# Three tiles begun at two changes of phase, norms' small products at fixed places, and the SSD's first group with its gates ahead of B and C

## The chip, the cores and the metric

The kernel runs on one core of a Trainium2 chip. The metric is the device time of one execution in microseconds (us); lower is better. A core has TensorE (PE, matrix products into PSUM), VectorE (DVE), ScalarE (ACT), GpSimd (POOL) and SyncE (SP), which issues the DMAs here. Each engine has a queue of its own and runs it in order; semaphores hold an instruction until what it reads is there.

## The reference

A backbone of two layers on 512 latent tokens and 256 context tokens, 1024 channels. Layer 0 mixes with attention, layer 1 with a bidirectional Mamba-2 state-space mixer (SSD); behind each comes a gated ConvFFN. Cut to what matters:

```python
for i in range(2):
    h_l = modulate(rms_norm(x, norm_mix_w[i]), mod_l[0], mod_l[1])      # the same for ctx
    o_l, o_c = attention_mixer(h_l, h_c, ...) if i == 0 else mamba2_mixer(h_l, h_c, ...)
    x = x + mod_l[2] * o_l                                              # ctx too in layer 0
    h_l = modulate(rms_norm(x, norm_ffn_w[i]), mod_l[3], mod_l[4])
    x = x + mod_l[5] * conv_ffn(h_l, ...)                               # ctx too in layer 0

def conv_ffn(h, w_up, conv_w, conv_b, w_down):
    g, u = jnp.split(h @ w_up, 2, axis=-1)
    g = dwconv_centred(g, conv_w, conv_b)
    return (jax.nn.silu(g) * u) @ w_down

# in mamba2_mixer
z, xbc, dt = jnp.split(h @ w_in, [D_INNER, D_INNER + CONV_DIM], axis=-1)
xbc = jax.nn.silu(dwconv_centred(xbc, conv_w, conv_b))                  # x, B and C
dt_f = jax.nn.softplus(dt_f + dt_bias_f)                                # dt_b likewise
# in ssd_scan, per chunk of 128 tokens
acs = jnp.cumsum(dtc * a, axis=2)
decay_end = jnp.exp(acs[:, :, -1:] - acs)
xw = xc * (decay_end * dtc)[..., None]
states = jnp.einsum('bcsgn,bcsgrp->bcgrpn', bc, xw)
```

## The kernel before, in words

Activations lie with channels on the partitions: a tile is 128 channels by tokens, and 1024 channels make 8 k-tiles. Tokens come in three segments: the context (256 columns), and the first and the second half of the latents (256 each). All products are float32 in three terms: activations and weights are split into a high half (`hh`, `wh`) and a low half (`hl`, `wl`), and `mm3` (L100) issues wh x hh (L105), wh x hl (L106) and wl x hh (L108) into one PSUM tile. A weight of 128 x 1024 is loaded by `load_w`: a DMA of 512 KB on SP's queue into `wst`, a cast on ScalarE that makes `wh` (L85), a subtraction on VectorE that makes `wl` (L87). `wst`, `wh` and `wl` share ten buffers, so a weight can be asked for only when an older one has been used up.

PSUM is cut into two tiles of 1024 columns (`S`) and four banks of 512 columns (`Bank`). GEMMs use `S`; down projections, the norms' small products and the first group's small steps use banks in turn.

A framework orders the instructions of each engine by its own estimate of when each is ready, program order deciding between equals; the queues then run in that order.

At a **change of phase** the last down projection of one phase (`down`, L952), the norm behind it (`Norm`, L345 on), and the first GEMMs of the next phase meet. For each segment and each of 8 output tiles m, `down` issues the products `ps_d` and a VectorE step X (L970) that adds gate times product to the residual; `Norm.sq` squares the new X on ScalarE and adds the squares. When a segment's eight are done, `Norm.gen` (L383) runs beside the next segment: the product with ones `ss` (L267), `rsa` on VectorE (L270), Ln and Exp on ScalarE (L272), two small steps `rsu` (L274, L275) and the row `rb` on VectorE (L278), then its transpose on TensorE (`rsT`, L284) and a copy `rs` on ScalarE (L394). Then `modulated` makes for each k-tile `ht` on VectorE (L312), the high half on ScalarE and the low half `hl` on VectorE (even k-tiles, L322) or, with two ScalarE steps, on GpSimd (odd ones, L317 to L319). `first_tiles` (L438) begins the two first GEMM tiles of the next phase in the two `S` tiles (`ps_first`): context and first latent half together, k by k for one tile and then the other, then the second half. Two such changes use it: from attention to layer 0's ConvFFN, whose first tiles are gate tile 0 and the up tile that goes with it (names ending in f), and from that ConvFFN to the SSD, whose first are the time steps dt and x tile 0 (names ending in s).

In the ConvFFN (`ffn`, L982) gate tile 1 is a GEMM of its own, 512 and 256 columns, in two banks (`ps_up1`).

The **SSD** (`ssd`, L1068) makes acs and dt from the first tile: Abs and Relu on ScalarE (L1106, L1107), then a chain on VectorE of exponentials' sums, a reciprocal, products and four scans (L1110 to L1128). It works in eight groups of six GEMMs (`inproj`): x, x, B, C, z, z. x, B and C are copied by ScalarE into a buffer `raw`, and go through a five-tap conv, four taps on VectorE (`xf`, `Bf`, `Cf`, L1152), and a Silu. Each group's state and outputs (`core`) are cut into steps that are taken while the next GEMMs run. Behind group 0's C come the transposes of acs and dt (`ps_dtT`, copied by VectorE into `acsT`, `dtT`, L1328), the product `ps_end` (L1333) that spreads each chunk's last value, and what hangs on them (`dec`, `dw`, `nacs`).

At the SSD's end `late_first` (L449) begins ConvFFN 1's first tiles behind the output projection with `Norm.chain`, which has one lag for both of its waits.

## Time and profile before

| what | us |
|---|---|
| median of 3 runs | 1902.2 (1901.54 to 1905.32) |
| the profiled execution | 1906.4 |
| its span | 1904.2 |
| TensorE busy in the span | 1864.1 |
| VectorE busy | 1331.0 |
| ScalarE busy | 845.4 |
| GpSimd busy | 256.9 |

The span runs from the first to the last instruction of the profiled execution. A row of the timeline gives start, duration, engine, line, operation, output and inputs; in square brackets stands the idle time of the engine ahead of it and what ended it. A row of a group ends with the same idle time summed. Products are pipelined: one of 256 columns is shown as 0.28 us, and the next starts before it ends. The mean granted clock of TensorE was 0.994 of full speed.

### The profile page before, as it was taken

The numbers are of one execution on the slowest core, as the hardware profiler recorded it, in microseconds if no ns is written. First come the engines' busy times: TensorE is split into PE (matmuls) and PEld (weight loads), VectorE is DVE, ScalarE is ACT, GpSimd is POOL, SyncE is SP. The second block draws the span as 40 slices with busy tenths as digits, with TensorE's granted clock in tenths as the row PEclk, the third lists the DMA queues.
The fourth block names the chain that finished last, engine by engine and source line by source line (L and its number), as shares of the span: only waits on it lengthen the run. The fifth ranks groups of instructions, "written<-read, shape, count | busy, mean of one in ns | idle before, by whom it ended". The sixth has DMA issues, their size and how long they took to land.

```text
span 1904.2 us, 27262 instructions
## 1 busy us (share of the span) xinstructions
PE 1864.1 (98%) x10696; PEld 1528.8 (80%) x10696; DVE 1331.0 (70%) x1983; ACT 845.4 (44%) x1454; POOL 256.9 (13%) x238
## 2 busy tenths in 40 slices
PE   8899999989999999999999999999999999999999
PEld 6774545578888888888888888888888888888887
DVE  4478889678877777544478777777878576565555
ACT  3645544355122222222256767766677352323331
POOL 2300000031000000000040334443334200000000
PEclk8999999999999999999999999999999999999999
DMA  9123341014334556221222344344343323323332
GB/s 339 56 67 97 118 157 40 23 56 166 122 122 133 163 189 186 72 67 56 67 89 80 116 122 122 114 131 123 116 130 119 100 78 101 101 86 111 89 99 89
DMA packets 73424, 210.00 MB, mean 110 GB/s; under 512 B 8912, under 2 KB 14416, under 8 KB 73168
## 3 DMA queue, kind: packets, MB, share of 16 engines
q1 hardware_dynamic: 73296, 208.26, 35.1%
q8 instruction: 84, 1.38, 0.3%
q14 instruction: 44, 0.36, 0.1%
HBM read 198.79 MB, written 6.82 MB: 108 GB/s over the span
## 4 chain that ended last, share of the span: by engine, by line
PE 79%; DVE 9%; issue 3%; ACT 3%; DMA 1%; POOL 1%; SPq 0%; DVEq 0%; POOLq 0%; ACTq 0%
PE ps_up L105 10%; PE ps_up L106 10%; PE ps_up L108 10%; PE ps_d L105 6%; PE ps_d L108 6%; PE ps_d L106 6%; PE ps_in L108 4%; PE ps_in L106 4%; PE ps_in L105 4%; PE ps_o L760 2%; PE ps_s L796 2%; PE ps_st L1222 2%; DVE ht L312 1%; PE ps_wo L108 1%; PE ps_wo L105 1%
## 5 line engine op out<-in xcount | busy, mean ns | idle before, releaser
L87 DVE TENSOR_TENSOR wl<-wst,wh 128x1024 fp32r<-128x1024 f32 x209 | 260.3, 1245 | 227.7 <-PE ps_up L106 121.6
L85 ACT CAST wh<-wst 128x1024 fp32r<-128x1024 f32 x211 | 221.2, 1049 | 422.0 <-DMA wst<-in_wup 321.6
L106 PE MATMUL ps_up<-hlf,wh 128*128 128x512 f32 x1008 | 357.2, 354 | 0.0
L108 PE MATMUL ps_up<-hhf,wl 128*128 128x512 f32 x1008 | 356.9, 354 | 0.0
L105 PE MATMUL ps_up<-hhf,wh 128*128 128x512 f32 x1008 | 356.7, 354 | 0.0
L105 PEld LDWEIGHTS ps_up<-hhf,wh 128*128 128x128 f32 x1008 | 190.6, 189 | 26.5
L106 PEld LDWEIGHTS ps_up<-hlf,wh 128*128 128x128 f32 x1008 | 190.7, 189 | 26.3
L108 PEld LDWEIGHTS ps_up<-hhf,wl 128*128 128x128 f32 x1008 | 190.6, 189 | 26.4
L105 PE MATMUL ps_in<-hhs,wh 128*128 128x512 f32 (+1 forms) x560 | 204.5, 365 | 0.0
L106 PE MATMUL ps_in<-hls,wh 128*128 128x512 f32 (+1 forms) x560 | 199.5, 356 | 0.0
L108 PE MATMUL ps_in<-hhs,wl 128*128 128x512 f32 (+1 forms) x560 | 198.8, 355 | 0.0
L105 PE MATMUL ps_d<-hdh,wh 128*128 128x512 f32 (+1 forms) x568 | 193.6, 343 | 1.4 <-DVE X L970 1.2
L108 PE MATMUL ps_d<-hdh,wl 128*128 128x512 f32 (+1 forms) x568 | 193.4, 341 | 0.0
L106 PE MATMUL ps_d<-hdl,wh 128*128 128x512 f32 (+1 forms) x568 | 193.0, 340 | 0.3 <-DVE hdl L87 0.3
L970 DVE SCALAR_TENSOR_TENSOR X<-ps_d,mod,X 128x512 f32<-128x512 f32 (+1 forms) x224 | 125.0, 584 | 34.1 <-PE ps_d L108 33.8
L106 PEld LDWEIGHTS ps_d<-hdl,wh 128*128 128x128 f32 x568 | 106.7, 188 | 14.8 <-DVE hdl L87 0.7
L105 PEld LDWEIGHTS ps_d<-hdh,wh 128*128 128x128 f32 x568 | 106.3, 188 | 14.8 <-DVE X L970 1.4
L105 PEld LDWEIGHTS ps_in<-hhs,wh 128*128 128x128 f32 x560 | 106.0, 189 | 15.1 <-issue 0.9
L108 PEld LDWEIGHTS ps_in<-hhs,wl 128*128 128x128 f32 x560 | 105.9, 189 | 14.8
L108 PEld LDWEIGHTS ps_d<-hdh,wl 128*128 128x128 f32 x568 | 106.7, 188 | 13.1
L106 PEld LDWEIGHTS ps_in<-hls,wh 128*128 128x128 f32 x560 | 106.0, 189 | 13.2
L799 ACT ACTIVATE pr<-ps_s 128x1024 f32<-128x1024 f32 x56 | 57.1, 1020 | 94.0 <-PE ps_s L798 86.7
(355 smaller groups left out, 3506.4 us busy)
## 6 DMA issues: line engine op xcount, KB each, us to landing
wst<-in_wup SPq DMA_DIRECT2D x88, 512.0 KB, 3.6
wada<-in_adaT SPq DMA_DIRECT2D x56, 512.0 KB, 3.7
wst<-in_win SPq DMA_DIRECT2D x48, 512.0 KB, 3.7
wst<-in_wdown SPq DMA_DIRECT2D x44, 512.0 KB, 3.7
E<-ad SPq DMA_DIRECT2D x64, 256.0 KB, 6.7
wada<-in_adaB SPq DMA_DIRECT2D x24, 512.0 KB, 5.0
ec<-ead SPq DMA_DIRECT2D x64, 128.0 KB, 5.1
wst<-in_wout SPq DMA_DIRECT2D x16, 512.0 KB, 3.6
```

The lines of the kernel that those rows point to most:

```text
L85: keep(nc.scalar.copy(hi, src))
L87: keep(eng.tensor_tensor(lo, src, _r(hi), ALU.subtract))
L105: mm(out, wh, ah, start=first, stop=False)
L106: mm(out, wh, al, start=False, stop=False)
L108: mm(out, wl, ah, start=False, stop=last)
L312: nc.vector.scalar_tensor_tensor(t[:, c0:c1], ap, g.moda[layer][ca][:, m, v : v + 1], rs[:, c0:c1], ALU.mult, ALU.mult)
L760: nc.tensor.matmul(po[S64[e], :n], v, pr[:, 512 * e + off : 512 * e + off + n], start=first, stop=last)
L796: nc.tensor.matmul(outs[e], a[S64[e], k], b[S64[e], q], start=i == 0, stop=False)
L799: nc.scalar.activation(pr, ps, AF.Exp)
L970: nc.vector.scalar_tensor_tensor(ap, o[:, c0:c1], gate[:, m, v : v + 1], ap, ALU.mult, ALU.add)
L1222: nc.tensor.matmul(ps[:, d * 256 : (d + 1) * 256], Bt[:, t * P : (t + 1) * P], xw[d][t], start=t == ts[0], stop=t == ts[-1])
```

## The change

1. `three_first` takes the place of `first_tiles`. Three tiles are begun: the two of before and gate tile 1 (ConvFFN 0) or x tile 1 (SSD), in two banks (`ps_first1`), whose weight is asked for at its start. It goes segment by segment, context first, and within a segment tile by tile. The last segment's norm runs in it by `Norm.chain`, its `ss` behind six k-steps and its `rsT` behind nine more, held there by `ordered` (an order without a semaphore). The rows of the latent halves are all made with the low half on VectorE.
2. `down` with a norm puts two output tiles into one bank (`ps_dn`), 256 columns each. The context's norm is as before; the first latent half's is a `chain` with a lag of 3 and 3.
3. `ffn` takes gate tile 1 from `first`.
4. `ssd`: dt's relu moves to VectorE (L1144) and Abs goes in three pieces; x tiles 0 and 1 are copied by `taken` at once. Group 0 runs z, z, then the transposes (`turned`), B's GEMM with `ends` behind its fourth k, x's taps, B's conv, C. Its `core` begins with one step and gives the others to group 1.
5. `Norm.chain` gets a second lag `then` (2 where nothing is given).

The core of the diff:

```diff
+def three_first(g, ws, norm, x, third):
+    ctx, la, lb = ending(norm.streams)
+    ws = ws + [load_w(g, third)]
+    tiles = [S(g, "ps_first") for _ in range(2)]
+    tiles = [[t[:, :L], t[:, L:T]] for t in tiles] + [[None, None]]
+    last = [None]
+    chain = norm.chain(LAST, 6, 9, lambda: last[0])
+    todo = {ctx: norm.rows(la, x), la: norm.rows(lb, x), lb: iter(())}
+    for seg in (ctx, la, lb):
+        i, a, b = seg
+        n = 0
+        for ps, w in zip(tiles, ws):
+            if ps[i] is None:
+                ps[i] = Bank(g, "ps_first1")[:, : (L, C)[i]]
+            for k in range(KT):
+                ks = slice(k * P, (k + 1) * P)
+                last[0] = mm3(g, (w[0][:, ks], w[1][:, ks]), [(ps[i][:, a:b], tuple(t[:, a:b] for t in norm.h[i][k]))],
+                              k == 0, k == KT - 1)
+                next(chain, None)
...
@@ down
-            ps = [(i, a, b, Bank(g, f"ps_d{i}")[:, : b - a]) for i, a, b in group]
+            if norm:
+                if m % 2 == 0:
+                    bank = Bank(g, "ps_dn")
+                ps = [(*group[0], bank[:, m % 2 * C : m % 2 * C + C])]
...
-            bg = norm.gen(group[0], x, 2)
-    return bg
+            bg = norm.gen(group[0], x, 2) if group[0][0] else norm.chain(group[0], 3, 3, lambda: last[0]) if group[0] != LAST else iter(())
@@ ssd, inproj
+        if gi == 0:
+            for j in range(2):
+                G.z.append(t2("z"))
+                nc.scalar.copy(G.z[j], gemm(ld(4 + j), (0,))[0])
+            turned()
+            ps = gemm(ld(2), (1, 0), ends)
+            G.x = [taps(*x) for x in x0]
...
+            G.B = conv(ps, 8 * 2, True, t3(g, "Bf"))
+            G.C = conv(gemm(ld(3), (0,)), 8 * 3, False, t2("Cf"))
```

What it moves, in the order of the instructions of an engine (a row: place, line, operation, output and inputs, shape).

TensorE in the second latent half of the down projection at the first change of phase; hhol and hlol are the attention's output, hhf_0 and on the normed k-tiles. Before:

```order
1486 L105 MATMUL ps_d_3961<-hhol_3588,wh 128x256
1487 L106 MATMUL ps_d_3961<-hlol_3589,wh 128x256
1488 L108 MATMUL ps_d_3961<-hhol_3588,wl 128x256
1489 L267 MATMUL ssf_3975<-ones,sqf_3890 128x1 x2
1490 L105 MATMUL ps_first<-hhf_0_3612,wh 128x256
1491 L106 MATMUL ps_first<-hlf_0_3613,wh 128x256
1492 L105 MATMUL ps_first<-hhf_0_3612,wh 128x256
1493 L106 MATMUL ps_first<-hlf_0_3613,wh 128x256
1494 L105 MATMUL ps_d_3988<-hhol_3220,wh 128x256
```

and now:

```order
1473 L108 MATMUL ps_dn<-hhol_3588,wl 128x256
1474 L105 MATMUL ps_first<-hhf_0_3612,wh 128x256
1475 L106 MATMUL ps_first<-hlf_0_3613,wh 128x256
1476 L108 MATMUL ps_first<-hhf_0_3612,wl 128x256
1477 L105 MATMUL ps_first<-hhf_1_3614,wh 128x256
1478 L106 MATMUL ps_first<-hlf_1_3615,wh 128x256
1479 L108 MATMUL ps_first<-hhf_1_3614,wl 128x256
1480 L105 MATMUL ps_first<-hhf_2_3616,wh 128x256
1481 L106 MATMUL ps_first<-hlf_2_3617,wh 128x256
1482 L108 MATMUL ps_first<-hhf_2_3616,wl 128x256
```

Where four products of the first tiles stood between two banks of the down projection, 21 stand now (rows 1474 to 1494), on k-tiles 0 to 6.

VectorE behind that down projection; `wl` is the third weight's low half now, the next GEMM's before, `rbf` the last segment's row. Before:

```order
461 L381 TENSOR_TENSOR sqf_4055<-sqf_4055,sqf_3945 128x256
462 L312 SCALAR_TENSOR_TENSOR ht<-X,moda_99,rsf_4016 128x256 x3
463 L322 SCALAR_TENSOR_TENSOR hlf_4_3605<-ht,mod_89,hhf_4_3604 128x256
464 L270 TENSOR_SCALAR rsa<-ssf_4119 128x2
465 L87 TENSOR_TENSOR wl<-wst,wh 128x1024
466 L322 SCALAR_TENSOR_TENSOR hlf_6_3609<-ht,mod_89,hhf_6_3608 128x256
467 L274 TENSOR_TENSOR rsu<-rsy,rsa 128x2
468 L275 SCALAR_TENSOR_TENSOR rsu<-rsy,rsu 128x2
469 L278 SCALAR_TENSOR_TENSOR rbf_4130<-rsu,rsy 128x256
```

and now:

```order
441 L322 SCALAR_TENSOR_TENSOR ht<-X,moda_99,rsf_4032 128x256
442 L389 TENSOR_TENSOR sqf_4030<-sqf_4030,sqf_4047 128x256
443 L391 TENSOR_TENSOR sqf_4030<-sqf_4030,sqf_3937 128x256
444 L332 SCALAR_TENSOR_TENSOR hlf_0_3597<-ht,mod_89,hhf_0_3596 128x256
445 L279 TENSOR_SCALAR rsa<-ssf_4084 128x2
446 L87 TENSOR_TENSOR wl<-wst,wh 128x1024
447 L283 TENSOR_TENSOR rsu<-rsy,rsa 128x2
448 L284 SCALAR_TENSOR_TENSOR rsu<-rsy,rsu 128x2
449 L287 SCALAR_TENSOR_TENSOR rbf_4095<-rsu,rsy 128x256
```

The norm's steps come behind one k-tile of the first latent half instead of most of them, and a `wl` still stands between `rsa` and `rsu`. On TensorE 14 products now lie between that norm's `ss` and its `rsT`.

VectorE at the SSD's start, from the last scans of acs to the copy of its transpose; `xf` rows are taps of the conv. Before:

```order
979 L1128 SCALAR_TENSOR_TENSOR acs<-dtu,dte 32x384
980 L1152 SCALAR_TENSOR_TENSOR xf<-raw_9259,par,xf 128x770
981 L87 TENSOR_TENSOR wl<-wst,wh 128x1024
982 L1152 SCALAR_TENSOR_TENSOR xf<-raw_9259,par,xf 128x770
983 L1152 SCALAR_TENSOR_TENSOR xf<-raw_9260,par,xf 128x770
984 L1152 SCALAR_TENSOR_TENSOR xf<-raw_9259,par,xf 128x770
985 L1152 SCALAR_TENSOR_TENSOR xf<-raw_9260,par,xf 128x770
986 L1152 SCALAR_TENSOR_TENSOR xf<-raw_9259,par,xf 128x770
987 L1152 SCALAR_TENSOR_TENSOR xf<-raw_9260,par,xf 128x770
988 L87 TENSOR_TENSOR wl<-wst,wh 128x1024
989 L1152 SCALAR_TENSOR_TENSOR xf<-raw_9260,par,xf 128x770
990 L1152 SCALAR_TENSOR_TENSOR Bf<-raw_9259,par,Bf 128x770 x2
```

and now:

```order
976 L1165 SCALAR_TENSOR_TENSOR acs<-dtu,dte 32x384
977 L1192 SCALAR_TENSOR_TENSOR xf<-raw_9327,par,xf 128x770
978 L1192 SCALAR_TENSOR_TENSOR xf<-raw_9328,par,xf 128x770
979 L1192 SCALAR_TENSOR_TENSOR xf<-raw_9327,par,xf 128x770
980 L1214 COPY acsT<-ps_dtT 128x3x2x64
981 L1214 COPY dtT<-ps_dtT 128x3x2x64
982 L1237 TENSOR_SCALAR nacs<-acsT 128x256
983 L1192 SCALAR_TENSOR_TENSOR xf<-raw_9327,par,xf 128x770
```

Before, the copy came behind all taps of x and two of B (its place is 991); now it comes behind three taps of x.

More of the change, by code (lines that the diff above doesn't have):

```diff
@@ L107, in mm3 @@
     for out, (ah, al) in outs:
-        mm(out, wl, ah, start=False, stop=last)
+        i = mm(out, wl, ah, start=False, stop=last)
+    return i
 def ada(g, src, layer, chunks, m0, nm, big=True):
@@ L251, in follow, with ordered, rstd_rows @@
     g.last_act = bi
+def ordered(g, bi, prev):
+    if prev is not None:
+        g.tc.add_manual_dep(bi.ins, prev.ins.name, mybir.DependencyInfo(
+            mybir.DependencyClass.NoSync, mybir.DependencyReason.DATA), reason="place among products")
 def ln_exp(g):
     follow(g, g.nc.scalar.preload_act_table_set("natural_log_exp_and_others"))
-def rstd_rows(g, sq, n, cols, width, name, bank):
+def rstd_rows(g, sq, n, cols, width, name, bank, behind=lambda: None):
     nc = g.nc
@@ L397, in gen, with chain @@
             yield
-    def chain(self, seg, lag=2):
+    def chain(self, seg, lag=2, then=2, behind=lambda: None):
         i, a, b = seg
@@ L405, in chain @@
             yield
-        rows = rstd_rows(g, self.acc[seg, 6], n, g.ones[:, :1], D, self.name, lambda nm: Bank(g, nm))
+        rows = rstd_rows(g, self.acc[seg, 6], n, g.ones[:, :1], D, self.name, lambda nm: Bank(g, nm), behind)
         next(rows)
-        for _ in range(lag):
+        for _ in range(then):
             yield
@@ L435, in firsts @@
     return [load_w(g, u) for u in units]
[L438 to L446 removed]
+def three_first(g, ws, norm, x, third):
[17 more added lines that the diff above has]
+                next(chain, None)
+                n += 1
+                if n > 4:
+                    next(todo[seg] if n % 2 else iter(()), None)
+        for _ in chain:
+            pass
+        for _ in todo[seg]:
+            pass
+    return tiles
 def late_first(g, ws, norm, x):
@@ L1052, in flush @@
             wf.extend(firsts(g, *after))
-        return down(g, ws, [acts.pop(f) for f in fs], gate, streams, x, order, norm, side=side)
+        down(g, ws, [acts.pop(f) for f in fs], gate, streams, x, order, norm, side=side)
     for fs in segs:
```

152 lines of the change are left out of this document (81 added, 71 removed).

## The prediction

> **What bounds the kernel now.** I read the page first, then the windows of the two changes of phase, then TensorE's groups in them, then single rows.
>
> ```profile
> span 1904.2 us, 27262 instructions
> ...
> PE 1864.1 (98%) x10696; PEld 1528.8 (80%) x10696; DVE 1331.0 (70%) x1983; ACT 845.4 (44%) x1454; POOL 256.9 (13%) x238
> ```
>
> TensorE (PE) is busy for 1864.1 of 1904.2 us, and no product is added or dropped in number of columns, so a change of order can only win TensorE's idle time back, or add to it. At most 40 us are idle in all, and this change touches four places. The windows of the two changes of phase (attention to ffn 0, ffn 0 to SSD) give start and end, the width, then PE's busy time:
>
> ```profile
> 408.00:446.00 38.00, 33.17 (x258) 1.00 0.18 59
> 968.00:1005.00 37.00, 31.85 (x249) 1.00 0.30 101
> ```
>
> So 38.00 - 33.17 = 4.83 us are idle in the first and 37.00 - 31.85 = 5.15 us in the second. TensorE's groups in them, the idle time ahead of each at the end of the row (first phase, then second):
>
> ```profile
> L105 PE MATMUL ps_d<-hhol,wh 128*128 128x256 f32 x48 | 13.9, 290 | 1.1 <-DVE X L970 1.1
> L106 PE MATMUL ps_first<-hlf,wh 128*128 128x256 f32 x48 | 13.6, 297 | 2.1 <-POOL hlf L319 1.5 <-DVE hlf L322 0.5
> L284 PE MATMUL rsTf<-cst,rbf 128*128 128x128 f32 x6 | 1.3, 291 | 1.2 <-DVE rbf L278 1.2
> ```
>
> ```profile
> L105 PE MATMUL ps_d<-hdh,wh 128*128 128x256 f32 x57 | 16.3, 286 | 1.2 <-DVE X L970 1.2
> L106 PE MATMUL ps_first<-hls,wh 128*128 128x256 f32 x46 | 13.0, 297 | 2.1 <-POOL hls L319 1.5 <-DVE hls L322 0.5
> L284 PE MATMUL rsTs<-cst,rbs 128*128 128x128 f32 x6 | 1.3, 291 | 1.3 <-DVE rbs L278 1.3
> ```
>
> Three kinds of wait: for a bank that VectorE (DVE) has not read (X), for the low halves of the normed activations (hl, most of it made by GpSimd), and for the norm's row rb. The other two places are in the SSD: the product that spreads the ends of the sums, and the last norm's first product.
>
> ```profile
> 1032.11 0.76 PE L1333 MATMUL ps_end<-acsT,cst 128*128 128x192 f32 x3 [0.90 <-DVE acsT L1328]
> ...
> 1535.06 0.60 PE L267 MATMUL ssf<-ones,sqf 128*128 128x1 f32 x4 [0.69 <-DVE sqf L381]
> ```
>
> Idle time within the reach of the change is thus 4.83 + 5.15 + 0.90 + 0.69 = 11.6 us, 0.6% of the span.
>
> **The change part by part.** The durations for all that follows. TensorE's step for a product of 256 columns:
>
> ```profile
> 407.02 0.28 PE L105 MATMUL ps_d<-hhol,wh 128*128 128x256 f32 x1
> 407.14 0.28 PE L106 MATMUL ps_d<-hlol,wh 128*128 128x256 f32 x1
> ```
>
> The same for 512 columns:
>
> ```profile
> 1019.72 0.39 PE L105 MATMUL ps_in<-hhs,wh 128*128 128x512 f32 x1
> 1019.95 0.39 PE L106 MATMUL ps_in<-hls,wh 128*128 128x512 f32 x1
> ```
>
> VectorE's step for X and ht, for wl and for the norm's row:
>
> ```profile
> 410.00 0.47 DVE L970 SCALAR_TENSOR_TENSOR X<-ps_d,mod,X 128x256 f32<-128x256 f32 x1
> 410.40 0.47 DVE L312 SCALAR_TENSOR_TENSOR ht<-X,moda,rsf 128x256 f32<-128x256 f32 x1
> ...
> 430.81 1.21 DVE L87 TENSOR_TENSOR wl<-wst,wh 128x1024 fp32r<-128x1024 f32 x1
> 431.95 0.96 DVE L322 SCALAR_TENSOR_TENSOR hlf<-ht,mod,hhf 128x256 fp32r<-128x256 f32 x1
> 432.83 0.70 DVE L274 TENSOR_TENSOR rsu<-rsy,rsa 128x2 f32<-128x2 f32 x1
> 433.75 0.42 DVE L278 SCALAR_TENSOR_TENSOR rbf<-rsu,rsy 128x256 f32<-128x256 f32 x1
> ```
>
> That is 0.12 us a narrow product, 0.23 a wide one, 0.40 a 256-column step of VectorE, 1.14 a wl, and 0.9 + 0.42 = 1.3 from rsu to the end of rb.
>
> (a) *The third tile.* Its 24 latent products were 512 wide; they now come as 48 of 256. 24 x (2 x 0.12 - 0.23) = 0.24 us more in each phase, **+0.5** in both. Nothing hides it.
>
> (b) *The waits for X and for rb of the first latent half* (1.1 + 1.2, 1.2 + 1.3). In the new order 21 products of the first tile's context columns (2.5 us) stand between the second latent half's first two tiles and its next ones, so X and rb have that long to come. I let these waits go, but for 0.2 us a phase. Behind it now stands the shared bank: the second half of each bank cannot begin before VectorE has read the first. By the order X of tile 6 has about 0.8 us (rsT and five products) and takes 0.28 + 0.47, which is just enough; ends 0 and 1.1 for each such place. The Trainium skill's page "PSUM — Partial Sum Buffer", section "PSUM bank collisions raise a hardware error", says that engines are to be kept apart by bank and not by address, which speaks against two tiles in one bank. By that rule each of the 12 second halves in a phase hangs on its X, no run here shows yet what that comes to, and the second rival below gives its time from rows.
>
> (c) *What is late next: the context columns' low halves.* The 21 products are asked for while VectorE still has X in hand. Odd tiles go through ScalarE twice and GpSimd:
>
> ```profile
> 413.13 0.51 ACT L317 ACTIVATE ht<-ht,mod 128x256 f32<-128x256 f32 x1
> ```
>
> ```profile
> 414.16 0.94 POOL L319 TENSOR_TENSOR hlf<-ht,hhf 128x256 fp32r<-128x256 f32 x1 [1.41 <-DVE ht L312]
> ```
>
> From ht to hl that is 414.16 + 0.94 - 413.13 = 2.0 us. Counting from the context's rsT, TensorE reaches the first tile after 41 products, 4.9 us. VectorE has ten steps up to ht 3, two of them behind TensorE's own products: about 5.2 us, hl 3 at 7.2, wanted at 6.6: 0.6. ht 5 is four steps on, hl 5 at 8.8, wanted at about 7.9: 0.9. **1.5 us** a phase, where the row of before has 1.5 for GpSimd too; ends 0 and the 2.1 of that row. For the latent columns VectorE now makes all low halves, 0.80 a k-tile: 19 steps with one wl (18 x 0.40 + 1.14 = 8.3 us) against 67 products (8.0): **0.4 us** with the sparse waits on the way, ends 0 and 1.0.
>
> (d) *The third weight.* It is asked for when a buffer falls free, six products ahead of the last down product (call the end of that T0), so at T0 - 0.7. The page's median from issue to landing:
>
> ```profile
> wst<-in_wup SPq DMA_DIRECT2D x88, 512.0 KB, 3.6
> ```
>
> The same for the SSD's weights between 984 and 990 us, where stores of X share the queue:
>
> ```profile
> DMA to landing us min/median/max: 3.9/4.2/4.5
> ```
>
> ScalarE's cast of a weight:
>
> ```profile
> 428.18 1.04 ACT L85 CAST wh<-wst 128x1024 fp32r<-128x1024 f32 x1
> ```
>
> With 3.6, wh stands in phase 1 at T0 + 4.0 and wl at T0 + 5.2. There the order puts ScalarE's cast ahead of the last norm's Ln and Exp, and VectorE's wl ahead of rsu and rb; before, too, but then nobody waited. rb comes at T0 + 6.5. TensorE has 15 products, the ss products (for which I take 0.35 us of waiting, half of the 0.69 of the row at 1535.06; ends 0 and 0.69) and 14 more: T0 + 4.4. It waits **2.0 us** for rb (1.7 to 2.3; 0 if the scheduler's order did not hold). In phase 2 Ln, Exp and rb stand ahead of cast and wl. With 4.2, wl comes at T0 + 3.5 + 1.04 + 1.2 = T0 + 5.8 or a little under and is wanted about seven products behind rsT, T0 + 5.3: **0.6 us** (0 to 1.4).
>
> So phase 1 idles 0.2 + 1.5 + 0.4 + 0.35 + 2.0 = 4.45 where it idled 4.83: **-0.4**. Phase 2 idles 0.2 + 1.5 + 0.4 + 0.35 + 0.6 = 3.05 where it idled 5.15: **-2.1**.
>
> (e) *The SSD's start.* The gates' chain on VectorE, first and last row, then a tap of the conv with the step behind it, and the copy that the product at 1032.11 waits for:
>
> ```profile
> 1007.54 0.36 DVE L1110 TENSOR_SCALAR dtu<-dte 128x384 f32<-128x384 f32 x1 [2.91 <-ACT dte L1108]
> ...
> 1018.66 0.95 DVE L1128 TENSOR_TENSOR_SCAN acs<-dtu,dte 32x384 f32<-32x384 f32 x1
> 1019.65 1.02 DVE L1152 SCALAR_TENSOR_TENSOR xf<-raw,par,xf 128x770 f32<-128x770 f32 x1
> 1020.59 1.22 DVE L87 TENSOR_TENSOR wl<-wst,wh 128x1024 fp32r<-128x1024 f32 x1
> ...
> 1031.51 0.55 DVE L1328 COPY acsT<-ps_dtT 128x384 f32<-128x384 f32 x1
> ```
>
> The chain takes 1019.61 - 1007.54 = 12.1 us. It begins about 0.6 us before the three tiles' end T1, since ScalarE copies x0 ahead of the last Abs, so acs stands at T1 + 11.5. TensorE has two z GEMMs, 48 x 0.23 = 11.0: 0.5 us of waiting. Then come the transposes (0.5) and 12 narrow products of B (1.4), and the ends' product wants acsT. That copy stands behind three taps on VectorE: 11.5 + 3 x 0.94 + 0.55 = T1 + 14.9 against T1 + 13.5: 1.4. C's wl stands behind eight taps and some small steps and may be 0.3 late. 2.2 in place of 0.90: **+1.3**; ends -0.9 (all in time) and +3 (another wl pushed in front). The relu on VectorE and the pieces of Abs cost ScalarE and VectorE some 0.3 us each ahead of T1, beside the third tile's products.
>
> (f) *The SSD's end.* Two steps between the last norm's products in place of what was there bring ss two products (0.24) forward, so it waits as much longer: **+0.2**, ends 0 and 0.5.
>
> The sum: +0.5 - 0.4 - 2.1 + 1.3 + 0.2 = **-0.5 us**. The profiled execution took 1906.4 us (its span of 1904.2 and 2.2 around it), 4.2 above the median of 1902.2 that is compared. I carry the difference over: **1901.7**.
>
> **The rivals.** *Waits vanish* (faster). All of (c), (d) and the 0.2 of (b) rest on VectorE and ScalarE being late by less than 1 us each but for one place. If they run 1 us ahead of my counts, 3.0 + 0.8 + 0.4 + 0.6 of waiting go, and 1 of the 2.0; 1901.7 - 5.8 = 1895.9. For it speaks that 32 low halves leave GpSimd's two-step path; against it that VectorE has 16 steps of 0.40 more in each phase and TensorE asks for the context columns sooner.
>
> *The shared banks bind* (slower). One mechanism: VectorE's X of a bank's first half queues behind norm rows, and the second half waits. The place is the last segment of each down projection, tiles 1, 3, 5 and 7; the price of one is the 1.1 to 1.2 of the ps_d rows. Two in each phase are 2 x (1.1 + 1.2) = 4.6: 1906.3; all four 1910.9. It decides once an X ends over 1.1 us (nine products) after its last product. For it speaks that VectorE has more to do here; against it the 21 products in between.
>
> *Group 1 is too full* (slower). The first group's state and outputs now fall into the second group's GEMMs. If their decay tiles come late, TensorE waits there, some 4 us: 1905.7. Against it: about 32 us of GEMMs lie between.
>
> That the change does not do what it says can be left out, since the order shows the third tile's products ahead of the ffn and the SSD.
>
> **How the numbers follow.** A measurement can tell about 0.2% (3.8 us) from no change. The forecast, 1901.7, has a chance of 0.55; its own range by the ends is 1898 to 1905. Waits vanish 0.27, shared banks 0.13, group 1 0.05. Faster by over 0.2% (under 1898.4): 0.27 and 0.03 from the forecast's end, 0.30. Slower (over 1906.0): both slower rivals, 0.18. The same: 0.52. For 8 in 10 the range goes from 1894.5, a little past the faster rival, to 1908, between the bank rival's two prices.
>
> **What would show it.** Right: at the first change of phase a wait of about 2 us at the last rsT for rb, GpSimd's low halves ahead of the first tile's context products, no X wait over 0.5; at the SSD's start a wait of over 1 us for acsT. Wrong: idle time in either phase below 1.5 us (first rival), or several waits for X at ps_dn (second), or idle time between 60 and 100 us behind the gates (third). The forecast falls if the phases' idle times differ from 4.5 and 3.1 by over 2 us.

## The result and the profile after

The changed kernel takes 1916.8 us (median of 6 runs, 1910.98 to 1919.07), the one before beside it 1903.8 (6 runs, 1901.54 to 1906.97). The ratio is 1.0062, with a 95% interval of 1.0049 to 1.0076: some 12 us slower. The forecast was 1901.7, with 1908.0 as the top of its range: it was wrong.

The page of the execution profiled after (it took 1914.02 us), its span and busy times:

```profile
span 1912.2 us, 27331 instructions
...
PE 1867.0 (98%) x10744; PEld 1531.0 (80%) x10744; DVE 1342.0 (70%) x2003; ACT 838.0 (44%) x1438; POOL 244.7 (13%) x222
```

TensorE's idle time is 1912.2 - 1867.0 = 45.2 us where it was 40.1. The windows of the two changes of phase come first: start and end, the width, then PE's busy time and products.

```profile
399.00:446.00 47.00, 44.22 (x347) 41.84 (x346) 37.21 (x85) 25.96 (x63) 15.42 (x19) 1.00 0.11 35
954.00:1008.00 54.00, 51.25 (x404) 48.52 (x404) 41.42 (x100) 28.76 (x69) 14.91 (x19) 1.00 0.24 78
```

They idle 2.78 and 2.75 us, where 4.45 and 3.05 were forecast and 4.83 and 5.15 stood before (in windows of 38 and 37 us). TensorE's waits in the first, with what ended each in brackets:

```profile
410.74 0.39 PE L105 MATMUL ps_dn<-hhol,wh 128*128 128x256 f32 x1 [0.34 <-DVE X L1005]
415.51 0.38 PE L106 MATMUL ps_first<-hlf,wh 128*128 128x256 f32 x1 [0.39 <-POOL hlf L329]
426.29 0.39 PE L108 MATMUL ps_first<-hhf,wl 128*128 128x256 f32 x1 [0.69 <-DVE wl L87]
431.70 0.44 PE L293 MATMUL rsTf<-cst,rbf 128*128 128x128 f32 x2 [1.18 <-DVE rbf L287]
```

These are the kinds that were forecast: X, the context's low halves, wl, and rb of the last norm. Now TensorE's waits at the SSD's start (the first row) and in group 1:

```profile
1025.56 0.92 PE L1220 MATMUL ps_end<-acsT,cst 128*128 128x192 f32 x4 [1.18 <-DVE acsT L1214]
...
1085.40 0.98 PE L1289 MATMUL ps_xt<-cst,xf 128*128 128x128 f32 x7 [2.01 <-DVE ec L1382]
1086.93 0.66 PE L1289 MATMUL ps_xt<-cst,xf 128*128 128x128 f32 x4 [0.55 <-DVE ec L1382]
1089.01 1.54 PE L1296 MATMUL ps_bt<-cst,Bf 128*128 128x128 f32 x6 [1.42 <-ACT Bf L1196]
1098.97 0.50 PE L108 MATMUL ps_in<-hhs,wl 128*128 128x512 f32 x1 [2.29 <-DVE wl L87]
```

Group 1 waits 6.3 us. The windows tell whose queue it is (PE, PEld, DVE, ACT and POOL busy, then the granted clock): of after, then of before, with the sum from 1080 to 1100 us.

```profile
1085.00:1090.00 5.00, 2.63 (x16) 2.16 (x17) 5.00 (x7) 2.58 (x5) 1.98 (x1) 0.84 0.97 278
1090.00:1095.00 5.00, 5.00 (x21) 4.11 (x20) 5.00 (x8) 3.14 (x5) 2.43 (x2) 0.82 0.13 48
```

```profile
1085.00:1090.00 5.00, 4.97 (x41) 3.91 (x41) 4.01 (x6) 2.65 (x5) 0.91 (x1) 1.00 0.37 108
1090.00:1095.00 5.00, 5.00 (x26) 4.18 (x25) 4.28 (x5) 2.84 (x5) 1.93 (x2) 1.00 0.03 7
...
sum 20.00, PE 19.97 PEld 16.63 DVE 18.29 ACT 9.91 POOL 5.65; mean PE 4.99 PEld 4.16 DVE 4.57 ACT 2.48 POOL 1.41
```

In before TensorE idles 0.03 us in 20. In after VectorE is busy without a gap, and behind the waits TensorE's granted clock is 0.84 and 0.82. A narrower window shows what stands behind these two means, one stretch at half speed:

```profile
1088.36:1091.77 3.41, 2.76 (x10) 2.47 (x11) 3.41 (x6) 1.46 (x3) 0.58 (x1) 0.50 0.69 257
```

TensorE works in it from 1089.01 on, so by an estimate it loses half of 2.8, 1.4 us more. VectorE's own rows there:

```profile
1081.88 1.01 DVE L1192 SCALAR_TENSOR_TENSOR Bf<-raw,par,Bf 128x770 f32<-128x770 f32 x1
1082.81 1.01 DVE L1192 SCALAR_TENSOR_TENSOR xf<-raw,par,xf 128x770 f32<-128x770 f32 x1
1083.74 1.01 DVE L1192 SCALAR_TENSOR_TENSOR Bf<-raw,par,Bf 128x770 f32<-128x770 f32 x1
1084.67 0.67 DVE L1382 TENSOR_TENSOR ec<-ec,ps_yo 128x512 f32<-128x512 f32 x1
1085.27 1.01 DVE L1192 SCALAR_TENSOR_TENSOR Bf<-raw,par,Bf 128x770 f32<-128x770 f32 x1
1086.20 0.67 DVE L1382 TENSOR_TENSOR ec<-ec,ps_yo 128x512 f32<-128x512 f32 x1
```

The step `ec`, which empties the bank that the transposes `ps_xt` want, stands behind taps of x and B. TensorE starts at 1085.40 and 1086.93, just behind the two `ec`.

To place the loss, I count from one mark, the first product on the context's columns in attention's down projections (308.46 before, 307.11 after; the last of these projections begins 82 us later), to the starts of some rows, in us:

| counted to | before | after | difference |
|---|---|---|---|
| ConvFFN 0's first down product | 187.5 | 186.1 | -1.4 |
| group 1's first ps_xt | 778.0 | 775.5 | -2.5 |
| group 2's first ps_xt | 832.9 | 838.7 | +5.8 |
| first ps_wo | 1124.8 | 1132.1 | +7.3 |
| ConvFFN 1's first down product | 1263.0 | 1272.4 | +9.4 |
| last product | 1592.2 | 1601.6 | +9.4 |

The two ends of group 1, of before and of after:

```profile
1086.49 0.66 PE L1196 MATMUL ps_xt<-cst,xf 128*128 128x128 f32 x4
...
1141.38 0.66 PE L1196 MATMUL ps_xt<-cst,xf 128*128 128x128 f32 x4
```

```profile
1082.59 0.33 PE L1289 MATMUL ps_xt<-cst,xf 128*128 128x128 f32 x1
...
1145.81 1.37 PE L1289 MATMUL ps_xt<-cst,xf 128*128 128x128 f32 x8
```

One round of group 1 takes 54.9 us before and 63.2 after: 8.3 us, the bulk of the loss. This **group 1 round** serves as a gauge below.

### The profile page after: what moved, and what is told of

Same layout as the page of the kernel before. It is cut to its first block, busy times and chain, and to the rows that moved or that the text cites. A ratio compares the mean times of both kernels' runs of the same rounds, so it can differ in the third digit from the quotient of the medians.

```text
span 1912.2 us, 27331 instructions
## 1 busy us (share of the span) xinstructions
PE 1867.0 (98%) x10744; PEld 1531.0 (80%) x10744; DVE 1342.0 (70%) x2003; ACT 838.0 (44%) x1438; POOL 244.7 (13%) x222
## 3 DMA queue, kind: packets, MB, share of 16 engines
q8 instruction: 84, 1.38, 0.3%
## 4 chain that ended last, share of the span: by engine, by line
PE 78%; DVE 10%; issue 3%; ACT 3%; DMA 2%; SPq 0%; POOL 0%; DVEq 0%; ACTq 0%; POOLq 0%
PE ps_up L105 10%; PE ps_up L106 10%; PE ps_up L108 10%; PE ps_d L105 6%; PE ps_d L108 5%; PE ps_d L106 5%; PE ps_in L108 3%; PE ps_in L106 3%; PE ps_in L105 3%; PE ps_o L789 2%; PE ps_s L825 2%; DVE xf L1192 2%; PE ps_st L1315 2%; PE ps_wo L106 1%; PE ps_wo L108 1%
## 5 line engine op out<-in xcount | busy, mean ns | idle before, releaser
L106 PE MATMUL ps_up<-hlf,wh 128*128 128x512 f32 x992 | 351.5, 354 | 0.0
L108 PE MATMUL ps_up<-hhf,wl 128*128 128x512 f32 x992 | 351.2, 354 | 0.0
L105 PE MATMUL ps_in<-hhs,wh 128*128 128x512 f32 (+1 forms) x544 | 198.8, 365 | 0.0
L108 PE MATMUL ps_d<-hdh,wl 128*128 128x512 f32 (+1 forms) x496 | 173.5, 350 | 0.0
L105 PE MATMUL ps_d<-hdh,wh 128*128 128x512 f32 (+1 forms) x496 | 173.3, 350 | 0.1
L106 PE MATMUL ps_d<-hdl,wh 128*128 128x512 f32 (+1 forms) x496 | 172.9, 349 | 0.0
L1005 DVE SCALAR_TENSOR_TENSOR X<-ps_d,mod,X 128x256 f32<-128x256 f32 (+1 forms) x176 | 102.5, 612 | 25.5 <-PE ps_d L108 25.2
L106 PEld LDWEIGHTS ps_d<-hdl,wh 128*128 128x128 f32 x496 | 93.2, 188 | 14.4 <-DVE hdl L87 0.2
L108 PEld LDWEIGHTS ps_d<-hdh,wl 128*128 128x128 f32 x496 | 93.1, 188 | 13.1
L105 PEld LDWEIGHTS ps_d<-hdh,wh 128*128 128x128 f32 x496 | 93.0, 188 | 13.0 <-ACT hdh L85 0.3
```

The lines of the kernel that those rows point to most:

```text
L105: mm(out, wh, ah, start=first, stop=False)
L106: mm(out, wh, al, start=False, stop=False)
L108: i = mm(out, wl, ah, start=False, stop=last)
L1005: nc.vector.scalar_tensor_tensor(ap, o[:, c0:c1], gate[:, m, v : v + 1], ap, ALU.mult, ALU.add)
```

## The experiments

The ratios are to the kernel before, run on the same chip, with 95% intervals. After stands at 1.0062. A difference of two ratios carries both intervals, some 3 us; so "+x by the trace" gives beside it how much later than in before the last product comes, counted from the mark, in the profiled execution. After stands at +9.4 there.

### Group 0 in its old order

```diff
-            if i == 0 or gi == 1 and i == 1:
+            if i == 0:
                 next(prev, None)
-            if gi == 1 and i == 0:
-                next(prev, None)
-            if i == 3 or gi == 0:
+            if gi == 0 and i == 3:
+                turned()
+                ends()
+            if i == 3:
```

(and group 0's own branch in `inproj` goes, with x's taps ahead of B and C.)

> Undoes the change's order of the SSD's first group alone: x0 and x1 (still begun at the change of phase) are conved first, then B, C, the gates' transposes and ends, z, z, with the core's steps from C on as in every other group. The three tiles, the shared banks and the placed norm products stay. If group 0's place is the cause of the whole loss, group 1's waits (2.0 + 0.55 + 1.42 + 2.29 us) and the clock below 1.00 go, and what is left are the phases' gains of about 3 us and a wait for acsT of 1 to 2.5 us: about 1901.5 (1899 to 1904) where before is 1903.8. If the three tiles or the shared banks cost time somewhere that the windows do not show, it stays over 1908.

Measured: 1912.53 us, 1.0027 [1.0014, 1.0040], +8.4 by the trace, and not the 1901.5 of the first alternative. The group 1 round is 54.9 us, so the crowding goes with the order. But the third tile has taken away x1's GEMM, 24 x 0.23 + 24 x 0.12 = 8.4 us, behind which the gates' chain used to run:

```profile
1030.89 1.33 PE L1220 MATMUL ps_end<-acsT,cst 128*128 128x192 f32 x3 [4.86 <-DVE acsT L1214]
```

The granted clock is 0.72 and 0.59 in the windows from 1026 and 1031 us. The change of group 0's order was there to fill a hole that the third tile makes; undone alone it gives at most a part of the time back. At the SSD's end, which the edit doesn't touch, this run also takes 3.7 us longer than before.

### Without the two GpSimd steps on group 0's decays

```diff
-                nc.gpsimd.affine_select(c4(e), c4(e), ...
+                if gi: nc.gpsimd.affine_select(c4(e), c4(e), ...
-                if d:
+                if d and gi:
                     nc.gpsimd.tensor_tensor(c4(e), c4(e), dtT ...
```

> The changed kernel, but for group 0 GpSimd's two steps on the decay tiles E (the mask and the product with dt) are left out, and ScalarE's exponential there reads another bias; group 0's outputs are not the reference's. If VectorE's queue is blocked by E tiles that come late from GpSimd (it sat idle for 2.3, 1.2, 0.5, 0.9, 2.0 and 0.9 us between 1060 and 1076), the taps behind them start earlier and 4 to 6 us of TensorE's 6.3 us of waiting in group 1 go: about 1909 to 1911. If VectorE simply has too much to do, the waits stay within 1.5 us: about 1915 to 1917.

Measured: 1911.89, 1.0039 [1.0025, 1.0052], +8.7 by the trace. Group 1 still waits 1.18 + 0.54 + 0.85 + 3.12 = 5.7 us, and its round is 61.7, 1.5 us under after's. GpSimd, for which VectorE idled ahead of the crowd, isn't the main cause.

### Without the taps of group 1's x tile 1 and B

```diff
-        for tap in (0, 1, 3, 4):
+        for tap in () if j in (3, 17) else (0, 1, 3, 4):
```

> The changed kernel, but the four taps of group 1's x tile 1 and of its B are left out (8 x 0.94 = 7.5 us of VectorE's time); group 1's outputs are not the reference's. If too much work on VectorE between 1075 and 1100 is the cause, nearly all of the 6.3 us of waits go: about 1908 to 1909. If the blocked queue is the cause, the work behind the block still shrinks and part goes too, but the first wait (2.0 us for ec, which stands behind these taps) alone would explain 2 to 3 us: about 1912 to 1914.

Measured: 1904.93, 0.9995 [0.9981, 1.0009], +1.1 by the trace. Of group 1's waits one of 0.47 us is left, the clock stays at 1.00, the round is 55.5. Eight taps, 7.5 us of VectorE, taken out of the queue give 7.8 us of TensorE back in that round: VectorE's queue is the cause.

### Group 0's core steps one at a time

```diff
-            if i == 0 or gi == 1 and i == 1:
+            if i == 0 or gi == 1 and i in (1, 3):
                 next(prev, None)
-            if gi == 1 and i == 0:
-                next(prev, None)
```

> The changed kernel with the five remaining steps of group 0's core handed out one to a place in group 1 (x0, x1, behind B's GEMM, behind C's GEMM, at C) instead of two at x0: the decay tiles are begun one GEMM later and y one GEMM later. If E tiles that come late block VectorE at y's time, y's move by one GEMM (8.4 us) gives them that time back and the waits at 1085 to 1099 go, some 4 to 6 us: about 1910 to 1912, unless group 2 takes them over. If VectorE is too full in group 1, the same work still stands there and group 1's core begins behind it: 1915 or more.

Measured: 1912.31, 1.0030 [1.0017, 1.0043], but +9.4 by the trace, as after. The waits move to the outputs (1.62 and 3.29 us at ps_y for E) and to group 2 (1.38 at ps_xt for ec). Spreading the steps moves the wait; it does not remove it.

### Products inside the wait

The first product of group 1's C GEMM, twelve times more:

```diff
+        for _ in range(again):
+            g.nc.tensor.matmul(ps[:, :L], w[0][:, :P], h[0][0][0], start=True, stop=True)
```

> The kernel after, with the first product of group 1's C GEMM issued twelve times more, 512 columns each, 12 x 0.23 = 2.8 us of TensorE work that changes no result. Theory (VectorE's queue sets when the transposes behind that GEMM may start, so 2.8 us more of products lie inside a wait, and the granted clock, which fell to 0.84 and 0.82 behind that wait, stays nearer 1): the wait ahead of ps_xt falls from 2.0 and 0.55 to 0.3 or less, the time is the same as after's or up to 1.7 us under it. Rival (TensorE's own length sets the time there): 2.8 us over after's.

Measured: 1912.33, 1.0043 [1.0026, 1.0059], +8.5 by the trace: 2.8 us of TensorE work put in, and the time is not longer than after's. In group 1 the theory holds: counted from the SSD's first GEMM, its first ps_cb comes at 90.1 us, 3.3 sooner than after's, with the 2.8 in. TensorE's own length doesn't set the time there. The clock is 1.00 from 1085 to 1095, and the waits shrink (1.26 at ps_xt, where 0.3 was expected, and 0.93 at ps_cb). But one of 5.49 us stands in group 2, for wl, and puts group 2's first ps_cb 3.4 us behind after's; so where the order of VectorE's queue is shifted, another wait shows up. That the whole is not longer is luck: the SSD's end, which the edit doesn't touch, takes 3.9 us less than in after.

### The first change of phase alone

The kernel before with `three_first` and after's down projection for attention to ConvFFN 0 only:

```diff
-    bg = down(g, ws, [g.oT[f] for f in (5, 6, 7)], ...)
-    first = first_tiles(g, wf, nrm, bg)
+    down_last(g, ws, [g.oT[f] for f in (5, 6, 7)], ...)
+    first = three_first(g, wf, nrm, x, I["wup"][0, 1])
```

> The kernel before, with the change at the first change of phase alone (three tiles from attention to ConvFFN 0, two tiles to a bank in that down projection, the norms' small products held at their places, gate tile 1 begun early). The second change of phase and the SSD are as before. Theory (the phases gain a little, the whole loss is in the SSD): TensorE idles some 2.8 us between the window's ends where it idled 4.83, group 1 has no wait that before lacks, and the time is 1 to 2 us under before's, a ratio of 0.9990 to 0.9997. Rival (the three tiles cost something behind the window, in the ConvFFN's buffers or the framework's order): a ratio of 1.001 or more, with new waits between 446 and 950 us.

Measured: 1903.0, 0.9995 [0.9983, 1.0006]. By the trace ConvFFN 0's first down product comes 1.3 us sooner than before's. A gain of the size expected, too small for the ratio to tell from none.

### Gates behind z 0, and then a bank for each tile

```diff
+        if gi == 0:
+            (x 0's taps, x 1's taps, z 0, turned, B with ends, C, z 1)
+            if gi == 0 and i == 4:
+                next(cur)
```

> The kernel after, but group 0 runs x0's taps, x1's taps, z 0, turned, B with the ends in its middle, C, z 1, and takes its core's steps from C on (one at C, two behind z 1, the rest in group 1 as the other groups do). Theory (group 0's postponed steps crowd VectorE in group 1; the run with group 0's old order lost only because nothing covered the gates' chain, 4.86 us): one z GEMM, 5.5 us, covers it, the wait at the ends' product is 1 us or less, group 1 has no wait over 0.6 and a clock of 1.00, and the time is before's within 3 us: 2 us from the phases, the SSD's end gives 2.2 back: a ratio of 0.998 to 1.001. Rival (the third tile itself, whose two sets of taps stand beside the gates' chain on VectorE, is what the SSD can't carry): 3 us or more of waits stay at ps_end, ps_st or in group 1, a ratio of 1.002 or more.

Measured: 1908.31, 1.0021 [1.0011, 1.0030]. Group 1 is clean (54.6), but one z GEMM is not cover enough: TensorE waits 1.92 us at ps_dtT and 2.69 at ps_end, with a clock of 0.85 and 0.80 behind. The rival's number is met. On top of it:

```diff
-                if m % 2 == 0:
-                    bank = Bank(g, "ps_dn")
-                ps = [(*group[0], bank[:, m % 2 * C : m % 2 * C + C])]
+                ps = [(*group[0], Bank(g, "ps_dn")[:, :C])]
```

> The kernel of the run before (gates behind z 0), with each tile of the down projections at the changes of phase in a bank of its own, 256 columns, where it shared one with its neighbour. Theory (the second half of a bank waits for VectorE's X of the first): the waits for X of 0.2 to 0.6 us in the phases go, 0.5 to 1 us a phase by the trace and 1 to 2 us in all, at most 0.1% and so hardly to be seen in the time. Rival (four banks in turn are then too few for two tiles and the norm's small products, the waits only move to the bank's next owner): the windows' idle time is the same or larger by up to 1 us.

Measured: 1899.81, 0.9974 [0.9962, 0.9986]. I had expected 1 to 2 us and got some 9. No theory of mine had this; so it was taken up by itself.

### After, with a bank for each tile

The last edit alone, on after.

> The kernel after with one edit: each tile of the two down projections ahead of the phases in a bank of its own. Theory (sharing a bank costs 3 to 4 us in each phase, as the two runs with the gates behind z 0 differ by 0.9974 and 1.0021; the crowding in group 1 is another cost, some 8 us, and stays): 7 to 9 us under after, a ratio to before of 1.001 to 1.003, with group 1's waits of some 6 us still there. Rival (the two costs are one, a late phase being what crowds group 1): group 1's waits go with the shared banks, a ratio of 0.996 to 0.998.

Measured: 1908.23, 1.0020 [1.0009, 1.0030], 8.0 us under after by the ratios and 5.4 by the trace. Both windows idle less, 0.96 and 1.53 us:

```profile
399.30:446.30 47.00, 46.04 (x379) 45.23 (x378) 39.87 (x89) 26.73 (x63) 14.44 (x17) 1.00 0.17 62
947.00:1001.00 54.00, 52.47 (x431) 51.14 (x430) 43.07 (x102) 29.98 (x71) 15.51 (x19) 1.00 0.27 89
```

The products tell more than the idle time: 379 and 431 in windows of the same width, where after has 347 and 404. Group 1's waits are all still there, and its round is 63.3:

```profile
1078.15 0.98 PE L1287 MATMUL ps_xt<-cst,xf 128*128 128x128 f32 x7 [2.02 <-DVE ec L1380]
1079.68 1.12 PE L1287 MATMUL ps_xt<-cst,xf 128*128 128x128 f32 x4 [0.55 <-DVE ec L1380]
1082.22 1.54 PE L1294 MATMUL ps_bt<-cst,Bf 128*128 128x128 f32 x6 [1.42 <-ACT Bf L1194]
1091.71 0.51 PE L108 MATMUL ps_in<-hhs,wl 128*128 128x512 f32 x1 [1.22 <-DVE wl L87]
```

So there are two costs, and they add up: the crowded group 1 some 8 us, and shared banks some 8, by the trace 7.5 up to group 1 (4.0 in the first phase and 3.5 in the second). The order of TensorE's queue in the first phase, as runs of products of one kind from the context's rsT to the last, shows why a shared bank costs so much while the waits for X are short. After, then with own banks:

```
rsT, ps_dn x42, ps_first x21, ps_dn x18, ss, ps_dn x27, rsT, ps_first x5, ps_dn x9, ps_first x15, ss, ps_first x13, rsT
rsT, ps_dn x63, ps_first x5, ss, ps_first x7, ps_dn x27, rsT, ps_dn x9, ps_first x19, ss, ps_first x23, rsT
```

With shared banks the framework's estimate holds the down tiles back and puts 26 of the next phase's products ahead of the last down products, before their low halves are there. With own banks 12 go ahead, and 42 in place of 28 are left to cover the last norm; its rb then waits 0.39 us and not 1.18. Counted from one product's start to the next (the last section shows how), the waits for X are some 1.2 of the 4 us; the rest stands at the low halves, at wl and at rb.

### The first phase alone, own banks

The kernel of "the first change of phase alone" with the same edit.

> The kernel with the first change of phase alone, own banks in its down projection; the second phase and the SSD as before. Theory (sharing costs 3.7 us in this phase by the trace): a ratio to before of 0.9965 to 0.998, 3 to 4.5 us under the run with the first phase alone and shared banks, and ConvFFN 0 starts some 5 us sooner than before's counted from the start of the last down projection. Rival (the gain of own banks came from the SSD's start, which a different phase 2 had shifted): a ratio of 0.9988 or more.

Measured: 1898.9, 0.9977 [0.9968, 0.9987], 3.4 us under the run with shared banks by the ratios; ConvFFN 0's first down product comes 5.8 us sooner than before's, 5.3 counted from the start of the last down projection (99.7 against 105.1). The SSD is before's there, so the rival falls.

### z 0 as the third tile

Own banks; the second phase begins group 0's z 0 in place of x 1.

```diff
-    ps_dt, *ps_x = three_first(g, wf, norm, x, g.I["win"][1])
+    ps_dt, ps_x0, ps_z0 = three_first(g, wf, norm, x, g.I["win"][4], (0,))
+            (group 0: x 0's taps, x 1, B, turned, C with ends, z 1; core from C on)
```

> A version meant to beat both: the phases with three tiles and own banks; the third tile of the second is group 0's z 0 (512 latent columns) in place of x tile 1; group 0 then runs x1, B, the turned gates, C with the ends in its middle, z 1, and its core's steps as the others but for two behind z 1. Theory (the phases give some 10 us, and the two GEMMs x1 and B, 16.8 us, cover the gates' chain as they did before; group 1 is as before): waits at ps_dtT and ps_end of 1 us or less, none in group 1 over 0.6, a ratio to before of 0.994 to 0.9965. Rival (the SSD can't take an earlier start, since VectorE's queue behind the gates is full whatever stands in front): waits of 4 us or more in groups 0 and 1, a ratio of 0.997 or more.

Measured: 1901.47, 0.9989 [0.9980, 0.9999]: short of what was expected. ps_end waits 0.74, ps_cb 1.77, and then one wait takes most of the gain, TensorE's at the start of group 2:

```profile
1121.68 0.58 PE L108 MATMUL ps_in<-hhs,wl 128*128 128x256 f32 x1 [5.49 <-DVE wl L87]
```

VectorE's rows ahead of it:

```profile
1112.27 1.02 DVE L1192 SCALAR_TENSOR_TENSOR xf<-raw,par,xf 128x770 f32<-128x770 f32 x1
1113.20 0.68 DVE L1388 TENSOR_TENSOR ec<-ec,ps_yo 128x512 f32<-128x512 f32 x1
1113.80 6.69 DVE L1192 SCALAR_TENSOR_TENSOR xf<-raw,par,xf 128x770 f32<-128x770 f32 x6
1120.41 1.21 DVE L87 TENSOR_TENSOR wl<-wst,wh 128x1024 fp32r<-128x1024 f32 x1
```

One weight's low half, 1.2 us of work, stands behind seven taps of the conv. What it reads was there by then: ScalarE's cast of that weight ended at 1112.90.

### Weights asked for one GEMM sooner

```diff
-        ld = lambda i: load_w(g, I["win"][6 * gi + i])
+        ld = lambda i: ahead(6 * gi + i)    # hands out the weight asked for last time, asks for the next
```

> The version with z 0 as the third tile, with each weight of the SSD's GEMMs asked for one GEMM sooner in the program, so that the framework puts group 2's weight (wl) ahead of six taps on VectorE that stood before it. No product, tap or load is added. Theory (TensorE's wait of 5.49 us in group 2 was wl's place in VectorE's queue, not VectorE's total work): that wait goes, a ratio to before of 0.995 to 0.997, 4 to 6 us under the version before. Rival (VectorE is full there, and whatever stands behind the weight is late next): waits of 3 us or more show up in group 2 at the transposes, a ratio of 0.998 or more.

Measured: 1895.24 (1894.27 to 1900.02), 0.9941 [0.9929, 0.9954]: 9 us under the version before by the ratios, 4.0 by the trace. The wait is gone, with the same work on VectorE; wl now stands behind one tap:

```profile
1109.84 1.02 DVE L1192 SCALAR_TENSOR_TENSOR xf<-raw,par,xf 128x770 f32<-128x770 f32 x1
1110.78 1.22 DVE L87 TENSOR_TENSOR wl<-wst,wh 128x1024 fp32r<-128x1024 f32 x1
1111.91 4.74 DVE L1192 SCALAR_TENSOR_TENSOR xf<-raw,par,xf 128x770 f32<-128x770 f32 x5
```

The span from group 1's first ps_xt to group 2's falls from 63.0 to 54.6 us; the trace shows less in the whole because the SSD's end takes 3.8 us longer. This version beats both kernels, by 0.6% and 1.2%. Whether the same edit alone would clear group 1 in after was not run.

### Two tiles in the second phase, the SSD as before

```diff
-    ps_dt, ps_x0 = first_tiles(g, wf, norm, bg)
+    ps_dt, ps_x0 = three_first(g, wf, norm, x)    # two tiles, own banks, no third
```

> The kernel with the first change of phase alone and own banks, and now the second change of phase in the new order too (segment by segment, small products held at their places, own banks), but with its two tiles of before and no third; the SSD's code and VectorE's order in it are as before. Theory (the gain of the phases comes from the order and the banks, the loss in the SSD from what the third tile and the postponed steps do to VectorE's queue): group 0 and 1 wait as before, 0.9 us at ps_end and nothing over 0.5 in group 1; the second phase gains 2 to 4 us over before's; a ratio to before of 0.9955 to 0.997. Rival (without the third tile's 48 or so products TensorE reaches the last segment before its norm and low halves are there): waits of 2 us or more at rsTs or at the low halves in the second phase, a ratio of 0.9975 or more.

Measured: 1898.45, 0.9953 [0.9940, 0.9967]. The second phase gains 3.5 us over before's (from ConvFFN 0's last down to the SSD's first GEMM, 50.2 against 53.7) without a third tile, and group 1 is clean (54.7). One wait of 1.35 us for ScalarE's reading of dt (L1182) has taken the third tile's place.

| kernel | ratio | by the trace | group 1 round |
|---|---|---|---|
| after | 1.0062 [1.0049, 1.0076] | +9.4 | 63.2 |
| after, own banks | 1.0020 [1.0009, 1.0030] | +4.0 | 63.3 |
| first phase alone, own banks | 0.9977 [0.9968, 0.9987] | -5.8 | 54.6 |
| both phases, two tiles in the second, own banks | 0.9953 [0.9940, 0.9967] | -7.2 | 54.7 |
| z 0 third, own banks | 0.9989 [0.9980, 0.9999] | -2.4 | 63.0 |
| the same, weights one sooner | 0.9941 [0.9929, 0.9954] | -6.4 | 54.6 |

Which of the two fastest is faster, these runs don't tell.

## Why the prediction was wrong, point by point

**The step that failed** is the last sentence on the rival "group 1 is too full": "Against it: about 32 us of GEMMs lie between." The sum carries no term for group 1 at all; the postponed steps of group 0 were taken as hidden. 32 us of TensorE's work do not cover anything if the engine that must do the steps is full. Before has VectorE busy for 18.29 of the 20 us from 1080 on, a row that I could have read, and the change adds steps there. The rival had the place right, its mechanism (late decay tiles) and its size (4 us) wrong, and a chance of 0.05. What it measured: 6.3 us of waits and some 1.4 of clock, an 8.3 us longer round. Leaving 7.5 us of taps out brings it back; leaving GpSimd's steps on the decays out does not.

By the table, in the terms of the sum: the phases -3.3 (forecast -2.0 with (a)), the SSD's start +0.8 (+1.3), group 1 +8.3 (no term), groups 2 to 7 +1.5 (no term), the SSD's end +2.1 (+0.2). That makes +9.4 where -0.5 was forecast.

**(a), the third tile's narrower products, +0.5.** Not seen by itself; the phases hold it.

**(b) to (d), the phases.** Forecast -0.4 and -2.1 of idle time, with (a) -0.2 and -1.9 of time. By the trace the first gained 1.4, where 0.2 was forecast. In the second, the time from ConvFFN 0's last down to the SSD's first GEMM is 60.14 us less x1's GEMM of 8.4, 51.74, against 53.68: 1.9. That the second's number is met is in part luck, since the terms did not all hold. rb waits 1.18 in the first where 2.0 was forecast, the context's low halves 0.39 where 1.5 was, and ss doesn't wait.

**The shared bank** was sized at 0.2 us a phase, and its rival at 4.6 for waits at X. In fact it costs 4.0 us in the first phase by the trace (186.1 against 182.1) and 8.0 in the whole by the ratios, and the waits for X are 0.37 and less. The waits that (c) and (d) priced for low halves and rb are largely its doing, by way of the order: I priced the effects and did not see the cause, since before has no kernel without sharing in the new order. The rule of the Trainium skill's "PSUM — Partial Sum Buffer", section "PSUM bank collisions raise a hardware error", that engines are kept apart by bank, spoke against this edit, and its sign was right. The mechanism of the rival (X behind norm rows) is not what the rows show.

**(e), the SSD's start, +1.3.** ps_end waits 1.18 and the transposes ahead of it 0.29, where 1.4 and 0.5 were forecast; 0.90 stood at ps_end before. The 0.3 for C's wl did not show. Up to group 1's first ps_xt the kernel is 2.5 us ahead, of the 1.4 + 1.9 = 3.3 that the phases won: 0.8 lost. Mechanism and sign right, the size 0.5 too high.

**(f), the SSD's end, +0.2.** From ps_wo to ConvFFN 1's first down product after loses 9.4 - 7.3 = 2.1 us: waits of 0.50 and 1.05 for yh and yl at ps_wo where before had one of 0.40, and 0.87 for hhf in place of ss's 0.69. The step that (f) prices isn't made: the last norm's `chain` has lags of 2 and 2 before and after, and only the norm of the first half goes from 1 and 1 to 1 and 2. In the run with products inside the wait ss waits 0.56 there and hhf doesn't, though the edit lies 450 us ahead: the framework's order follows its estimates. With the same code in that stage, it takes 136 to 142 us in the changed kernels' runs. What in the estimate decides it stays open. Of the 1.5 us between group 2 and ps_wo the most is a wait of group 1's kind, 1.39 us for ec at group 3's ps_xt, and one of 0.69 for xf at group 4's.

**The rival "waits vanish"** needed under 1.5 us of idle time in a phase. After has 2.8 in each; with own banks they have 0.96 and 1.53. It is the way the phases would have gone with one edit less.

The trace's 9.4 us and the ratio's 12 (9.3 to 14.5 by the interval) agree at the interval's edge; the other runs of after had mean granted clocks of 0.990 to 0.996, the profiled one 0.993.

## What to carry to other kernels

Work that is moved "behind" TensorE's products is hidden only if the engine that does it has room in that very stretch: read that engine's windows at the place it goes to, and what stands behind it in its queue. A small step that TensorE needs (a weight's low half, the emptying of a bank) belongs ahead of long steps that nobody waits for; one place sooner in program order was worth 8.4 us of a round of 63.0 here. Where a framework orders the queues, a shared buffer can cost more by the order that it makes than by waits for that buffer: run it once with and once without sharing.

## What the runs showed of the hardware

The granted clock falls behind waits, and what the products then lose adds to the wait. In these traces it is 1.00 or 0.50, and behind the SSD's waits the slow stretches last 3.4 or 6.8 us; a value between is the mean of a window that holds part of one. Around a wait of 4.86 us (group 0 in its old order) it was 0.72 and 0.59; with 2.02, 0.55 and 1.42 us of waiting within 6 us (own banks on after) it was 0.50 and 0.86:

```profile
1080.00:1085.00 5.00, 3.58 (x14) 2.89 (x13) 5.00 (x7) 2.58 (x5) 1.69 (x1) 0.50 0.66 227
1085.00:1090.00 5.00, 5.00 (x21) 4.07 (x20) 5.00 (x5) 1.88 (x3) 4.68 (x4) 0.86 0.00 0
```

How long a wait is does not settle it. With 1.18, 0.54 and 0.85 us and then 3.12 (no GpSimd steps) the clock stayed at 1.00; behind a single wait of 1.92 us (a bank for each tile on the gates behind z 0) it was 0.50. The windows behind the 3.12 and behind the 1.92:

```profile
1098.00:1103.00 5.00, 4.62 (x20) 3.86 (x21) 2.85 (x4) 2.05 (x3) 0.82 (x1) 1.00 0.39 87
```

```profile
1019.14:1022.54 3.40, 3.40 (x10) 2.63 (x9) 3.40 (x5) 0.82 (x1) 0.00 (x0) 0.50 0.61 155
```

The Trainium skill's page "TensorE: Matmul & The Clock Gate", section "What's actually happening", names an idle window of about 3.4 us after which the clock drops. These rows agree only in part: the clock dropped 2.2 us into the wait of 4.86 (1.00 in the window from 1026.04 to 1028.23, 0.50 in that from 1028.24 to 1030.88), and behind waits that were shorter than such a window.

A wait costs TensorE more than the idle time in brackets. Ahead of 410.74 in after the products start 0.12 us apart; then 0.62 us pass from one start to the next (410.12 to 410.74), and 0.22 to the one behind. That is 0.50 + 0.10 = 0.6 us lost where the bracket says 0.34. Likewise, with the first phase alone and own banks 5.3 us were won from the last down projection's start to ConvFFN 0's first down product, while the idle time in a window of 47 us fell by 4.1, from 4.93 to 0.80 (the row of before, then that run's):

```profile
400.30:447.30 47.00, 42.07 (x328) 39.79 (x328) 39.12 (x81) 28.78 (x69) 21.69 (x25) 1.00 0.18 59
```

```profile
396.00:443.00 47.00, 46.20 (x381) 45.39 (x379) 39.64 (x89) 26.91 (x63) 14.23 (x17) 1.00 0.19 66
```
